# Feed-forward lots of 2, 6, 6 and 8 tiles: both lots of six go down by seven block products, the first lot over all eight banks

## The chip, the cores and the metric

The kernel runs on one core of one Trainium2 chip. The metric is the device time of one execution in microseconds. Before the change it was 1090.71 us (median of three runs, 1090.43 to 1090.75).

## The reference

The reference is a two-layer transformer trunk on one sequence of 512 tokens, 1024 wide, with a memory of 256 rows. Each layer is a token mixer with memory attention, and then a feed-forward part of hidden width 2816. All inputs are fp32, and layer 1 has another mixer than layer 0. What the change touches is the feed-forward part:

```
for i in range(DEPTH):                       # 2 layers
    ...                                      # mixer A (i = 0) or B (i = 1), memory attention, W_o
    h = rms_norm(x, g_ffn_pre[i])
    gu = h @ w_gate_up[i]                    # 512x1024 @ 1024x5632
    f = (jax.nn.silu(gu[..., :D_FF]) * gu[..., D_FF:]) @ w_down[i]   # D_FF = 2816
    x = x + rms_norm(f, g_ffn_post[i])
```

## The kernel before

An fp32 number is held as two rounded parts, hi and lo, in a format that TensorE (PE) multiplies fast; each product of matrices is three matmuls, hi by hi, hi by lo and lo by hi (`mm3`, lines 307 to 309). Every weight block is loaded as fp32 into a raw buffer by a DMA on SyncE's queue (SP) and split on the chip: ScalarE (ACT) rounds the hi part (`split`, line 317), VectorE (DVE) subtracts it to get the lo part (line 321). Such a block of 128x1024 is called a unit (`unit`).

The hidden width is cut into 22 tiles of 128 (f = 0 to 21). Tiles 0 and 1 compute gate and up as plain products. Every other tile does so by seven block products instead of eight (Strassen's scheme with Winograd's sums, `seven`, lines 1143 to 1145), each matmul 128x256; `prep_a` to `prep_d` and `load_b` load, add and split the weights for them one to three tiles ahead. For the "far" tiles some of the weight sums are made by DMAs that GpSimd (POOL) issues with an accumulate (`load_far`, `add`), which saves DVE work.

The hidden tiles are multiplied with `w_down` in lots: `LOTS` = tiles 0 to 7, 8 to 13 and 14 to 21, and each lot's result is added to `o` (four tiles of 128x1024, in SBUF). The lots go down in three ways:

- lot 0 (eight tiles): `Trunk.down`, eight products per token tile for each half of the output columns, in four banks of PSUM at a time, 192 matmuls of 128x512 (the first of them between the lot's last gate/up products); ACT copies the result to `o`.
- lot 1 (six tiles, `SEVEN` = 1): `down` in `ffn`, seven block products A11, A12, S2, S1, S3, S4, A22 in this order, by `times` (lines 1255 to 1257), 126 matmuls of 128x512. Its weights come as blocks b11, b12, b21, b22 of `ws`, 128x1536 each, in two pieces (1024 columns in `raw`, `ru` or `rb`, 512 in `rs`). The sums t1 to t4 of blocks are made by loads on SP and accumulates of POOL (`load_block`, `add`, line 1091). `down_load` issues all of them in four steps: 0 and 1 while the lot's last tiles run, 2 at the start, 3 after product A12. `pairs` splits a block for PE, `out_of` adds a finished product to `o` on DVE (line 1265).
- the last lot (eight tiles): `ffn_out`, 192 matmuls again, with the post norm.

`ahead` is called eight times in `Trunk.down` (after each unit) and four times in `ffn_out`. It takes one item of a list `todo`, a weight unit that the next layer's mixer will need, loads and splits it and, at the next call, stores both parts to DRAM (`pair`). In the next layer `unit` fetches the parts instead of loading and splitting again. The list has eight items (four of `wq`, then four of `wo`). It is filled in layer 0 before the feed-forward; six items are prepared in layer 0, and the two left over are prepared in layer 1's first lot, where nothing uses them.

PE's instructions run in the order of the program text. The order on the other engines and on the DMA queues is chosen by a scheduler at build time and is fixed in the program; `queue` ties one DMA behind the last one that was tied on the same queue (`issue_after`). Each engine works strictly in that order: an instruction that waits holds up everything behind it on its engine, and a DMA that waits to be issued holds up its queue.

Of the kernel before, what the change touches and what calls it, by code (L numbers as in the profile page):

```python
# [9 lines left out]
F32 = mybir.dt.float32  # L10
# [6 lines left out]
P = 128  # L17
# [43 lines left out]
def _pack(w_in, w_mem_kv, w_o, w_gate_up, w_down):  # L61
    wkv = np.empty((DEPTH, 4, P, 768), np.float32)
    wq = np.empty((DEPTH, 4, 2, P, 1024), np.float32)
    wm = np.empty((DEPTH, 4, P, 1024), np.float32)
    wo = np.empty((DEPTH, 2, KD // 2, P, 1024), np.float32)
    wgu = np.empty((DEPTH, NF, 2, P, 1024), np.float32)
    wd = np.empty((DEPTH, 2, NF // 2, P, 1024), np.float32)
    ws = np.empty((DEPTH, 2, 2, P, HALF * 512), np.float32)
    qk = NH * HD + NG * HD
    cols = (np.arange(0, qk, HD)[:, None] + AXIAL[None, :]).reshape(-1)  # L70
    w_in = w_in.copy()
    w_in[1, :, :qk] = w_in[1][:, cols]
    for l in range(DEPTH):
        for u in range(4):
            wkv[l, u] = _unit_layout(w_in[l], 2 * u, 2, 768, 384)
            wm[l, u] = _unit_layout(w_mem_kv[l], 2 * u, 2, 0, 512)
        for c in range(4):
            c0 = 256 * c if c < 3 else 1152
            for u in range(2):
                wq[l, c, u] = _unit_layout(w_in[l], 4 * u, 4, c0, 256)  # L80
        for h in range(2):
            for u in range(KD // 2):
                wo[l, h, u] = _unit_layout(w_o[l], 2 * u, 2, 512 * h, 512)
            for u in range(NF // 2):
                wd[l, h, u] = _unit_layout(w_down[l], 2 * u, 2, 512 * h, 512)
            for z in range(2):
                ws[l, z, h] = _unit_layout(w_down[l], LOTS[SEVEN][0] + HALF * z, HALF, 512 * h, 512)
# [115 lines left out]
class Trunk:  # L203
# [492 lines left out]

    def axial(self, buf):
# [4 lines left out]
        nc.sync.dma_start(buf[:, :2 * NT * HD], a["ropeb"])  # L702
        nc.sync.dma_start(buf[:, 2 * NT * HD:2 * NT * HD + 2 * HD], _rows(a["qk_norm_g"], 2 * HD))
        nc.gpsimd.tensor_scalar(g[:, 0], g[:, 0], -(HD ** -0.5), 1.0, op0=OP.mult, op1=OP.mult)
        for z in range(2):
            nc.gpsimd.tensor_mul(self.gt[:, z, 0], rt[:, 0], g[:, z, None, :].to_broadcast([P, NT, HD]))
            for h in range(2):
                o, i = slice(32 * h, 32 * h + 32), slice(32 - 32 * h, 64 - 32 * h)
                nc.gpsimd.tensor_mul(self.gt[:, z, 1, :, o], rt[:, 1, :, o],
                                     g[:, z, None, i].to_broadcast([P, NT, 32]))  # L710

# [187 lines left out]

    def down(self, get, w, fs, c, o, head=None):  # L900

        nc = self.nc
        for h in range(2):
            ps = head["ps"] if h == 0 else [self.tagged(z) for z in ("s", "pv", "acc", "acc")]
            for u in range(len(fs) // 2):
                wu = head["w"] if (h, u) == (0, 0) else self.unit(w[h, fs[0] // 2 + u])
                for t in range(0 if h or u else 2, NT):
                    self.down_prod(ps[t], get, fs, u, t, wu)
                self.ahead()
            for t in range(NT):  # L910
                z = o[t][:, 512 * h:512 * h + 512]
                if c == 0:
                    nc.scalar.activation(z, ps[t], AF.Copy)
                else:
                    nc.vector.tensor_add(z, z, ps[t])

    def down_prod(self, ps, get, fs, u, t, wu):
# [78 lines left out]
    def ffn(self, l, pools, forms, late, done):  # L996
# [26 lines left out]
        def keep_hidden(f, s, i, lot):  # L1023
            p = F[f] = hidden(i)
            a, b = slice(0, 256), slice(256, 512)
            if lot != SEVEN or i >= HALF:
# [20 lines left out]

            if lot == SEVEN:
                forms_due.append(low if i < HALF else high)
# [4 lines left out]

        def block(name, z, i, t):
            f0 = LOTS[SEVEN][0]
# [7 lines left out]
        def product(f):  # L1064
            if f < 2:
                return o[2 + f][:, :512]
            return temp("k" if 0 <= f - LOTS[SEVEN][0] < HALF else "s")

# [17 lines left out]
        def far(f):  # L1086
            return 1 < f - LOTS[SEVEN][0] < 2 * HALF

# [160 lines left out]

        def times(ps, name, pr, steps, fresh):  # L1250
            mm = nc.tensor.matmul
            for i, t in steps:
                lh, ll = block(name, 0, i, t), block(name, 1, i, t)
                rh, rl = [pr[i // 2][z][:, i % 2 * 512:i % 2 * 512 + 512] for z in range(2)]
# [12 lines left out]
        def down_load(h, step):  # L1267
            (b11, b12), (b21, b22) = [[self.a["ws"][l, z, n] for n in range(2)] for z in range(2)]
            if step == 0:
# [12 lines left out]
        def down_begin(h):  # L1282
            h["x"] = [self.tagged("acc"), self.tagged("acc")]
            h["w"] = pairs(h["b11"])
            down_load(h, 2)
            times(h["x"], "A11", h["w"], BY_UNIT[:4], True)

        def down(h):
# [10 lines left out]
            times(x, "S2", w, BY_UNIT, False)  # L1299
# [6 lines left out]
            times(x, "S3", w, BY_ROW, False)  # L1306
            out_of(x, 1, 1, True)
            w = pairs(h["b22"])
            times(y, "S4", w, BY_ROW, False)
            out_of(y, 0, 1)  # L1310
            w = pairs(h["t4"])
            times(x, "A22", w, BY_ROW, False)
            out_of(x, 1, 0)

        for c, (f0, f1) in enumerate(LOTS):
            fs = list(range(f0, f1))
            get = lambda z, k, t, f0=f0: F[f0 + k][z][:, t * P:(t + 1) * P]
            gs = [f for f in fs if f >= 2]
            if c:
                prep_a(gs[0])  # L1320
# [8 lines left out]
            prep_d(gs[0])  # L1329
            head = {}  # L1330

            def begin(nxt, nxt2):
                if c == SEVEN and nxt == fs[-1]:
                    down_load(head, 1)
                if c == SEVEN and nxt2 == fs[-1]:
                    down_load(head, 0)

            def first():
                if c == SEVEN:
                    down_begin(head)  # L1340
                    return
# [4 lines left out]
            def second():  # L1346
                if c == SEVEN:
                    times(head["x"], "A11", head["w"], BY_UNIT[4:], True)
                    return
# [6 lines left out]
            if c == SEVEN:  # L1356
# [225 lines left out]
```

## Time and profile before

The profile is of one execution of 1090.64 us; the span from its first to its last instruction is 1088.9 us, so 1.7 us lie outside the span.

| what | measured |
|---|---|
| median of three runs | 1090.71 us |
| profiled execution, its span | 1090.64 us, 1088.9 us |
| PE, DVE, ACT, POOL busy | 1066.2, 867.5, 677.5, 228.7 us |
| feed-forward lot 0, layer 0 and 1 | 104.42 and 101.16 us |
| feed-forward lot 1 (six tiles), layer 0 and 1 | 86.30 and 86.32 us |

How to read it: PE stands for matmuls, SPq for SyncE's DMA queue, a row of the timeline is the start, the length, the engine, the line of the program, the operation and out<-in. In the view of waits a row names who waited for what, then the microseconds in all, how often, and the longest. In a view of DMAs the last number is the median time from issue to landing. Times are counted from the start of the span.

### The profile page before, as it was taken

Reading aid. Unit: us, or ns where it says so; the run is one execution under the profiler, and the core shown is the slowest. Engines: PE = TensorE matmul, PEld = TensorE weight load, DVE = VectorE, ACT = ScalarE, POOL = GpSimd, SP = SyncE. Lnnn points to the kernel's source line nnn. Section 1 sums busy time; section 2 is a strip of 40 time slices with the busy share of each in tenths; the row PEclk is TensorE's granted clock in tenths of the full one; section 3 lists DMA queues with packets and bytes.
Section 4 is the critical chain, followed back from the end, with each engine's and each line's share of the span. In section 5 each row is a group of like instructions: output and inputs, shape, how many; then the busy total and the mean of one; then the engine's idle time right before and its main releaser. Section 6 shows DMA issues by size and latency. Waiting matters only on the chain.

```text
span 1088.9 us, 19743 instructions
## 1 busy us (share of the span) xinstructions
PE 1066.2 (98%) x7400; PEld 976.6 (90%) x7400; DVE 867.5 (80%) x1489; ACT 677.5 (62%) x1393; POOL 228.7 (21%) x373
## 2 busy tenths in 40 slices
PE   9999999999999999999999999999999999999997
PEld 7899878999789989997898888778999899899986
DVE  7789875999557989985888988767997468899954
ACT  7679974765445646654567888756664356556631
POOL 5773331102001100001444543312000001100001
PEclk9999999999999999999999999999999999999999
DMA  9721007333865972338732220145135648833243
GB/s 337 255 78 39 23 20 264 124 98 129 268 205 146 259 204 89 117 118 305 240 131 97 78 78 20 59 154 193 62 117 204 182 117 248 226 117 101 72 158 116
DMA packets 48624, 159.23 MB, mean 146 GB/s; under 512 B 5649, under 2 KB 6033, under 8 KB 48401
## 3 DMA queue, kind: packets, MB, share of 16 engines
q1 hardware_dynamic: 43632, 147.09, 40.0%
q0 software_dynamic: 4608, 10.49, 5.6%
q8 instruction: 58, 0.95, 0.4%
q10 hardware_dynamic: 288, 0.40, 0.1%
q14 instruction: 38, 0.30, 0.1%
HBM read 135.94 MB, written 18.87 MB: 142 GB/s over the span
## 4 chain that ended last, share of the span: by engine, by line
PE 78%; DVE 9%; ACT 5%; DMA 3%; issue 2%; POOL 2%; SPq 0%; DVEq 0%; POOLq 0%; ACTq 0%
PE ps L1144 11%; PE ps L1143 11%; PE ps L1145 11%; PE ps L308 10%; PE ps L307 10%; PE ps L309 10%; PE tp L672 3%; PE ps L1257 2%; PE ps L1256 2%; PE ps L1255 2%; PE o L686 2%; PE o L687 2%; DVE wlo L321 2%; ACT whi L317 1%; PE s L611 1%
## 5 line engine op out<-in xcount | busy, mean ns | idle before, releaser
L317 ACT ACTIVATE whi<-raw 128x512 fp32r<-128x512 f32 (+3 forms) x198 | 159.9, 826 | 122.5 <-DMA pair<-whi 30.3
L321 DVE TENSOR_TENSOR wlo<-raw,whi 128x512 fp32r<-128x512 f32 (+3 forms) x194 | 180.0, 943 | 64.0 <-ACT whi L317 59.7
L1144 PE MATMUL ps<-hrows,wlo 128*128 128x256 f32 x640 | 176.3, 276 | 0.0
L1143 PE MATMUL ps<-hrows,whi 128*128 128x256 f32 x640 | 176.2, 275 | 0.0
L1145 PE MATMUL ps<-hrows,whi 128*128 128x256 f32 x640 | 176.2, 275 | 0.0
L307 PE MATMUL ps<-whi,hrows 128*128 128x256 f32 (+2 forms) x432 | 143.8, 333 | 0.0
L308 PE MATMUL ps<-wlo,hrows 128*128 128x256 f32 (+2 forms) x432 | 137.7, 319 | 1.6 <-DVE wlo L321 1.6
L309 PE MATMUL ps<-whi,hrows 128*128 128x256 f32 (+2 forms) x432 | 137.6, 319 | 0.0
L1143 PE MATMUL ps<-a,whi 128*128 128x256 f32 x480 | 132.2, 275 | 0.5 <-DVE c L1179 0.5
L1144 PE MATMUL ps<-a,wlo 128*128 128x256 f32 x480 | 132.1, 275 | 0.0
L1145 PE MATMUL ps<-a,whi 128*128 128x256 f32 x480 | 132.1, 275 | 0.0
L1143 PEld LDWEIGHTS ps<-hrows,whi 128*128 128x128 f32 x640 | 120.1, 188 | 0.5
L1144 PEld LDWEIGHTS ps<-hrows,wlo 128*128 128x128 f32 x640 | 120.1, 188 | 0.5
L1145 PEld LDWEIGHTS ps<-hrows,whi 128*128 128x128 f32 x640 | 120.1, 188 | 0.0
L308 PE MATMUL ps<-wlo,f 128*128 128x512 f32 (+1 forms) x264 | 101.6, 385 | 2.4 <-DVE wlo L321 2.4
L307 PE MATMUL ps<-whi,f 128*128 128x512 f32 (+1 forms) x264 | 101.3, 384 | 0.3 <-ACT whi L317 0.3
L309 PE MATMUL ps<-whi,f 128*128 128x512 f32 (+1 forms) x264 | 101.1, 383 | 0.0
L662 POOL TENSOR_SCALAR p<-p,rd 128x256 f32<-128x256 f32 (+2 forms) x128 | 78.2, 631 | 101.4 <-DVE rd L659 59.3
L1143 PEld LDWEIGHTS ps<-a,whi 128*128 128x128 f32 x480 | 90.1, 188 | 0.9 <-DVE c L1179 0.7
L1144 PEld LDWEIGHTS ps<-a,wlo 128*128 128x128 f32 x480 | 90.1, 188 | 0.2
L1145 PEld LDWEIGHTS ps<-a,whi 128*128 128x128 f32 x480 | 90.1, 188 | 0.0
L308 PEld LDWEIGHTS ps<-wlo,hrows 128*128 128x128 f32 x432 | 81.4, 188 | 7.5 <-DVE wlo L321 2.5
(229 smaller groups left out, 2663.2 us busy)
## 6 DMA issues: line engine op xcount, KB each, us to landing
raw<-in_wgu_dram SPq DMA_DIRECT2D x48, 512.0 KB, 4.5
rb<-in_wgu_dram SPq DMA_DIRECT2D x40, 512.0 KB, 3.7
raw<-in_wd_dram SPq DMA_DIRECT2D x32, 512.0 KB, 4.8
raw<-in_wo_dram SPq DMA_DIRECT2D x18, 512.0 KB, 3.6
raw<-in_wq_dram SPq DMA_DIRECT2D x16, 512.0 KB, 4.9
xt<-x SPq DMA_DIRECT2D x12, 512.0 KB, 5.0
raw<-in_wm_dram SPq DMA_DIRECT2D x8, 512.0 KB, 4.2
x<-y SPq DMA_DIRECT2D x8, 512.0 KB, 2.9
```

Source lines behind the costliest of these rows:

```text
L307: mm(out, lh, rh, start=first, stop=False)
L308: mm(out, lh, rl, start=False, stop=False)
L309: mm(out, ll, rh, start=False, stop=last)
L317: a = nc.scalar.activation(hi, src, AF.Copy)
L321: b = nc.vector.tensor_sub(lo, src, hi.bitcast(F32))
L662: self.pooled = nc.gpsimd.tensor_scalar(hd["p"][z][:, :n], hd["p"][z][:, :n], rd[:, z:z + 1], 1.0, op0=OP.mult, op1=OP.mult)
L672: nc.tensor.transpose(tp[:, z], hd["p"][i][:, jj * P:(jj + 1) * P], self.ident)
L686: nc.tensor.matmul(o[:, c0:c1], hd["v"](j), th, start=(j == 0), stop=False, skip_group_check=True)
L687: nc.tensor.matmul(o[:, c0:c1], hd["v"](j), tl, start=False, stop=last, skip_group_check=True)
L1143: mm(out, wh[:, s], rh, start=start and k == 0, stop=False, skip_group_check=True)
L1144: mm(out, wl[:, s], rh, start=False, stop=False, skip_group_check=True)
L1145: mm(out, wh[:, s], rl, start=False, stop=k == 3, skip_group_check=True)
```

## The change

The lots become tiles 0 and 1, 2 to 7, 8 to 13 and 14 to 21, and both lots of six go down by seven products. `ws` holds the blocks of both.

The new first lot is done at once behind the plain tiles. It needs two units of `w_down`, one for each half of the columns, which are loaded and split while the plain tiles run (`w0`). Its 48 matmuls go over all eight banks of PSUM, four token tiles by two halves, tile 0 first and tile 1 after it, and ACT copies the eight results to `o`. The preparation of tile 2 (`prep_a(2)`) and the second half of the token sums (`forms.finish(1)`) stand after the plain tiles now. `Trunk.down` is gone.

With it go eight of the calls of `ahead`. In their place `down` calls a new function `spare` twice, after step 3 of `down_load` and after product S1. The first call takes an item of `todo`, queues its load on SP into a raw buffer behind what is queued there, and splits it in two halves (into `c` and `s`, buffers of 128x512 that the gate/up tiles use otherwise); the second queues the four stores. In layer 0's first way down by seven the first call also queues two loads of the rope tables for layer 1 (`axial`, which stood behind lot 0 before). The four calls in `ffn_out` stay. So four items are prepared in layer 0 and four in layer 1, the last two of those in `ffn_out`.

```diff
-LOTS = ((0, 8), (8, 14), (14, 22))
-SEVEN, HALF = 1, 3
+LOTS = ((0, 2), (2, 8), (8, 14), (14, 22))
+SEVEN, HALF = (1, 2), 3
...
             act(f, pgs[f])
             if f == 0:
+                raw0 = wide("ru")
+                nc.sync.dma_start(raw0, self.a["wd"][l][0, 0])
+                w0 = [self.unit(self.a["wd"][l][0, 0], raw=raw0)]
                 forms.finish(0)
-                prep_a(2)
-                forms.finish(1)
+                w0.append(self.unit(self.a["wd"][l][1, 0]))
+        prep_a(2)
+        forms.finish(1)
+        get = lambda z, k, t: F[k][z][:, t * P:(t + 1) * P]
+        ps = [[self.tagged(z) for z in tags.split()] for tags in ("t t acc acc", "s s s pv")]
+        for k in range(2):
+            c = slice(512 * k, 512 * k + 512)
+            for h in range(2):
+                for t in range(NT):
+                    self.mm3(ps[h][t], get(0, k, t), get(1, k, t), w0[h][0][:, c], w0[h][1][:, c], k == 0, k == 1)
+        for h in range(2):
+            for t in range(NT):
+                nc.scalar.activation(o[t][:, 512 * h:512 * h + 512], ps[h][t], AF.Copy)
...
+        def spare():
+            if l == 0 and "rope" not in turn:
+                turn["rope"] = 1
+                self.axial(tmp.tile([P, 10 * HD], F32, tag="rope", name="rope", bufs=1), queue, ends)
+            if self.stores:
+                for dst, src in self.stores:
+                    queue(nc.sync, dst, src)
+                self.stores = []
+            elif self.todo:
+                name, *at = self.todo.pop(0)
+                x = self.wraw.tile([P, 1024], F32, tag="raw", name="raw", bufs=3)
+                queue(nc.sync, x, self.a[name][tuple(at)])
...
+                for z in range(2):
+                    c = slice(512 * z, 512 * z + 512)
+                    hi, lo = temp("c"), temp("s")
+                    self.split(hi.bitcast(F32R), lo.bitcast(F32R), x[:, c])
+                    self.stores += [(y[0][:, c], hi), (y[1][:, c], lo)]
...
-            times(z, "A12", w, BY_UNIT, True)
+            times(z, h, "A12", w, BY_UNIT, True)
             down_load(h, 3)
+            spare()
             out_of(z, 0, 0)
...
-            times(y, "S1", w, BY_ROW, True)
+            times(y, h, "S1", w, BY_ROW, True)
+            spare()
             out_of(y, 1, 1)
...
             if c == SEVEN:
                 down(head)
-            elif c < len(LOTS) - 1:
-                self.down(get, self.a["wd"][l], fs, c, o, head)
-                if l == c == 0:
-                    self.axial(wide("ru"))
```

(The last `if` reads `if c in SEVEN` now, as its like elsewhere.) In the changed kernel the line numbers move: the splits of DVE are line 322, the loads of `queue` line 1079, `out_of` line 1267, the three matmuls of `times` lines 1257 to 1259.

The first place where the order moves is SP's queue at the end of a lot of six. Before, in layer 0, from the last loads of `ws` on (`raw<-in_wgu` and `rb<-in_wgu` are for the next lot's tiles; the last `rs` is the second half of b22, the row ahead of it b22's first half or t4):

```order
L1091 DMA rb<-in_ws_dram 128x1024
L1109 DMA raw<-in_wgu_dram 128x1024 x3
L1091 DMA rs<-in_ws_dram 128x512
L1091 DMA rb<-in_ws_dram 128x1024
L1091 DMA rs<-in_ws_dram 128x512
L1091 DMA rb<-in_ws_dram 128x1024
L1091 DMA rs<-in_ws_dram 128x512
L1113 DMA rb<-in_wgu_dram 128x1024 x4
```

After, the same place of the second lot of six in layer 0:

```order
L1079 DMA rb<-in_ws_dram 128x1024
L1079 DMA rs<-in_ws_dram 128x512
L1079 DMA rb<-in_ws_dram 128x1024
L1079 DMA rs<-in_ws_dram 128x512
L1079 DMA rb<-in_ws_dram 128x1024
L1079 DMA rs<-in_ws_dram 128x512
L1079 DMA raw<-in_wq_dram 128x1024
L1097 DMA raw<-in_wgu_dram 128x1024 x2
L1079 DMA pair<-c 128x512
L1101 DMA rb<-in_wgu_dram 128x1024
```

The three loads for the next lot no longer stand among the `ws` loads; the spare's load and two of them stand behind the last one. In layer 1 both lots of six read the same way (with `wo` for `wq`); in layer 0's first lot of six the two rope loads stand between the last `rs` and the spare's load.

The second place is DVE during the way down, from the split of t3 (`wlo<-rb`, `wlo<-rs`) to that of b22. Before, in layer 0:

```order
L321 TENSOR_TENSOR wlo<-rs,whi 128x512
L1265 TENSOR_TENSOR o<-o,ps 128x512 x2
L321 TENSOR_TENSOR wlo<-rb,whi 128x1024
L321 TENSOR_TENSOR wlo<-rs,whi 128x512
L1265 TENSOR_TENSOR o<-o,ps 128x512 x2
L321 TENSOR_TENSOR wlo<-rb,whi 128x1024
L321 TENSOR_TENSOR wlo<-rs,whi 128x512
L1265 TENSOR_TENSOR o<-o,ps 128x512
```

After, in the second lot of six of layer 0 (`s<-raw,c` are the spare's two half splits):

```order
L322 TENSOR_TENSOR wlo<-rs,whi 128x512
L1267 TENSOR_TENSOR o<-o,ps 128x512 x2
L322 TENSOR_TENSOR wlo<-rb,whi 128x1024
L322 TENSOR_TENSOR s<-raw,c 128x512 x2
L1267 TENSOR_TENSOR o<-o,ps 128x512
L322 TENSOR_TENSOR wlo<-rs,whi 128x512
L1267 TENSOR_TENSOR o<-o,ps 128x512
L322 TENSOR_TENSOR wlo<-rb,whi 128x1024
L322 TENSOR_TENSOR wlo<-rs,whi 128x512
L1267 TENSOR_TENSOR o<-o,ps 128x512
```

The spare's splits stand ahead of the second half of t3, which product S3 reads in its third step. In layer 1 both lots of six have the same order; in layer 0's first lot of six the spare's splits stand behind both halves of t3 and ahead of b22.

More of the change, by code (lines that the diff above doesn't have):

```diff
@@ L695, in value, with axial @@
         nc.vector.tensor_add(self.tok[here, hg // 2], o[here], tmp[here])
-    def axial(self, buf):
+    def axial(self, buf, queue, ends):
         nc, a = self.nc, self.a
@@ L701, in axial @@
         g = buf[:, 2 * NT * HD:2 * NT * HD + 2 * HD].rearrange("p (z d) -> p z d", d=HD)
[L702 to L704 removed]
+        queue(nc.sync, buf[:, :2 * NT * HD], a["ropeb"])
+        queue(nc.sync, buf[:, 2 * NT * HD:2 * NT * HD + 2 * HD], _rows(a["qk_norm_g"], 2 * HD))
+        with self.tc.issue_after(ends[nc.gpsimd]):
+            last = nc.gpsimd.tensor_scalar(g[:, 0], g[:, 0], -(HD ** -0.5), 1.0, op0=OP.mult, op1=OP.mult).ins
         for z in range(2):
[L706 removed]
+            with self.tc.issue_after(last):
+                last = nc.gpsimd.tensor_mul(self.gt[:, z, 0], rt[:, 0], g[:, z, None, :].to_broadcast([P, NT, HD])).ins
             for h in range(2):
                 o, i = slice(32 * h, 32 * h + 32), slice(32 - 32 * h, 64 - 32 * h)
[L709 to L710 removed]
+                with self.tc.issue_after(last):
+                    last = nc.gpsimd.tensor_mul(self.gt[:, z, 1, :, o], rt[:, 1, :, o],
+                                                g[:, z, None, i].to_broadcast([P, NT, 32])).ins
+        ends[nc.gpsimd] = last
     def mixer(self, l, mkp, late, tokp):
@@ L898, in mix_out @@
         return late
[L900 to L915, printed above, removed]
     def down_prod(self, ps, get, fs, u, t, wu):
@@ L1025, in keep_hidden @@
             a, b = slice(0, 256), slice(256, 512)
-            if lot != SEVEN or i >= HALF:
+            if lot not in SEVEN or i >= HALF:
                 self.flo = signed(p, slice(0, 512), s)
@@ L1046, in high @@
                 signed(F["S4", q // 2], (a, b)[q % 2], r[:, a])
-            if lot == SEVEN:
+            if lot in SEVEN:
                 forms_due.append(low if i < HALF else high)
@@ L1053, in due, with block @@
                 forms_due.pop(0)()
-        def block(name, z, i, t):
-            f0 = LOTS[SEVEN][0]
+        def block(lot, name, z, i, t):
+            f0 = LOTS[lot][0]
             key, h = {"A11": (f0 + i, 0), "S3": (f0 + i, 1), "A12": (f0 + HALF + i, 0), "A22": (f0 + HALF + i, 1),
@@ L1086, in far @@
         def far(f):
-            return 1 < f - LOTS[SEVEN][0] < 2 * HALF
+            return any(1 < f - LOTS[c][0] < 2 * HALF for c in SEVEN)
         def queue(eng, *args, **kw):
@@ L1248, in pairs, with times @@
             return out
-        def times(ps, name, pr, steps, fresh):
+        def times(ps, h, name, pr, steps, fresh):
             mm = nc.tensor.matmul
             for i, t in steps:
-                lh, ll = block(name, 0, i, t), block(name, 1, i, t)
+                lh, ll = block(h["lot"], name, 0, i, t), block(h["lot"], name, 1, i, t)
                 rh, rl = [pr[i // 2][z][:, i % 2 * 512:i % 2 * 512 + 512] for z in range(2)]
@@ L1267, in down_load @@
         def down_load(h, step):
-            (b11, b12), (b21, b22) = [[self.a["ws"][l, z, n] for n in range(2)] for z in range(2)]
+            (b11, b12), (b21, b22) = [[self.a["ws"][l, SEVEN.index(h["lot"]), z, n] for n in range(2)] for z in range(2)]
             if step == 0:
@@ L1285, in down_begin @@
             down_load(h, 2)
-            times(h["x"], "A11", h["w"], BY_UNIT[:4], True)
+            times(h["x"], h, "A11", h["w"], BY_UNIT[:4], True)
+        def spare():
[10 more added lines that the diff above has]
+                queue(nc.sync, x, self.a[name][tuple(at)])
+                self.pairs[(name, *at)] = y = [self.dram.tile([P, 1024], F32, name="pair", tag="_".join(map(str, (name, z, *at))))
+                                               for z in range(2)]
+                for z in range(2):
[3 more added lines that the diff above has]
+                    self.stores += [(y[0][:, c], hi), (y[1][:, c], lo)]
         def down(h):
@@ L1329, in ffn @@
             prep_d(gs[0])
-            head = {}
+            head = dict(lot=c)
             def begin(nxt, nxt2):
-                if c == SEVEN and nxt == fs[-1]:
+                if c in SEVEN and nxt == fs[-1]:
                     down_load(head, 1)
-                if c == SEVEN and nxt2 == fs[-1]:
+                if c in SEVEN and nxt2 == fs[-1]:
                     down_load(head, 0)
             def first():
-                if c == SEVEN:
+                if c in SEVEN:
                     down_begin(head)
@@ L1346, in second @@
             def second():
-                if c == SEVEN:
-                    times(head["x"], "A11", head["w"], BY_UNIT[4:], True)
+                if c in SEVEN:
+                    times(head["x"], head, "A11", head["w"], BY_UNIT[4:], True)
                     return
```

23 lines of the change are left out of this document (12 added, 11 removed).

## The prediction, on record before the result was known

> **What bounds the kernel now.** I read the page's busy times, its clock line and the chain of waits first.
>
> ```profile
> span 1088.9 us, 19743 instructions
> PE 1066.2 (98%) x7400; PEld 976.6 (90%) x7400; DVE 867.5 (80%) x1489; ACT 677.5 (62%) x1393; POOL 228.7 (21%) x373
> PEclk9999999999999999999999999999999999999999
> PE 78%; DVE 9%; ACT 5%; DMA 3%; issue 2%; POOL 2%; SPq 0%; DVEq 0%; POOLq 0%; ACTq 0%
> ```
>
> TensorE (PE) sets the end: 98% busy at full clock, 78% of the chain. A matmul less is worth its pitch, as long as VectorE (DVE), ScalarE (ACT) and the loads keep up. So I went to the stages that change. The view of windows gives, in this order, the first lot and the lot of six in layer 0, then the same two in layer 1, then the last 14 us of the plain tiles and the six-tile lot's way down in layer 0.
>
> ```profile
> core 0: us, PE busy (x) PEld busy (x) DVE busy (x) ACT busy (x) POOL busy (x), PEclk, DMA share, GB/s
> 220.97:325.39 104.42, 102.05 (x699) 93.39 (x698) 78.54 (x102) 51.87 (x82) 9.44 (x10) 1.00 0.57 183
> 325.39:411.69 86.30, 86.30 (x632) 80.80 (x632) 72.38 (x113) 50.40 (x84) 11.42 (x13) 1.00 0.73 196
> 774.32:875.48 101.16, 101.16 (x699) 93.34 (x698) 74.47 (x100) 50.61 (x80) 2.68 (x3) 1.00 0.49 154
> 875.48:961.80 86.32, 86.32 (x632) 80.80 (x632) 71.58 (x113) 50.41 (x84) 11.48 (x13) 1.00 0.72 196
> 207.00:221.00 14.00, 14.00 (x125) 14.00 (x124) 14.00 (x23) 11.39 (x19) 0.00 (x0) 1.00 0.13 39
> 387.00:411.70 24.70, 24.70 (x110) 20.15 (x109) 23.03 (x34) 11.59 (x16) 2.67 (x3) 1.00 0.64 173
> ```
>
> Both lots of six tiles take 86.3 us with PE never idle. The first lot of layer 0 loses 2.4 us (104.42 against 102.05 busy); the waits of PE in that window name most of it:
>
> ```profile
> PE ps L308 <- DVE wlo L321: 1.6, 2, 0.8
> PE ps L1143 <- DVE c L1179: 0.5, 1, 0.5
> PE ps L307 <- ACT whi L317: 0.3, 1, 0.3
> ```
>
> **The change, part by part.** *The first lot.* Today it is six seven-way tiles plus 192 matmuls of 128x512 down. It becomes 48 such matmuls for tiles 0 and 1, and six tiles that go down as the lot of six does now. One such matmul costs, from the first and last starts of the lot of six's way down in PE's timeline (108 matmuls of lines 1255 to 1257 between the first row and the last, which begins the next lot):
>
> ```profile
> 386.74 0.39 PE L1255 MATMUL ps<-whi,f 128*128 128x512 f32 x1
> 411.53 0.28 PE L1143 MATMUL ps<-a,whi 128*128 128x256 f32 x1
> ```
>
> (411.53 - 386.74)/108 = 0.2295 us. The 48 take 48 x 0.2295 = 11.0 us, and the six tiles another 86.3: 97.3 us in place of 104.42 (layer 0: -7.1) and of 101.16 (layer 1: -3.9), **-11.0 us** together. By count it is 36 matmuls less, 36 x 0.2295 = 8.3 us; the other 2.7 us are layer 0's stalls and slack inside the windows. The 48 need two weight splits more on DVE. What covers them: DVE is full before the lot (14.00 of 14.00 us), but the 11.0 us of matmuls need no other DVE work, so the backlog that now sits ahead of tile 2 has that time to drain. The eight copies to `o` are ACT's, which was busy 51.87 of 104.42 us. I take no stall there. Without the cover it is at most the two splits, 2 x 1.22 us per layer (the 128x1024 split is quoted below).
>
> *The spare work inside the sevens.* This is the dear part. Eight next-layer weight units used to be pre-split between the units of the ordinary way down; now `spare` does one inside each way down by seven products. The order shows that the load of the spare unit (`raw<-in_wq`) stands on SP right behind `rs<-in_ws`, the second half of block b22. Today that row waits on SP for a long time: the waits of SP (layer 0, then layer 1), and the rows of SP, PE, POOL and the DMA view around it.
>
> ```profile
> SPq L1091 <- DMA rs<-rs: 11.1, 1, 11.1
> SPq L1091 <- DMA rs<-rs: 11.9, 1, 11.9
> 383.79 0.33 SPq L1091 DMA_DIRECT2D rb<-in_ws_dram  x1
> 385.92 0.33 SPq L1091 DMA_DIRECT2D rs<-in_ws_dram  x1
> 386.34 0.39 SPq L1091 DMA_DIRECT2D rb<-in_ws_dram  x1
> 397.94 0.33 SPq L1091 DMA_DIRECT2D rs<-in_ws_dram  x1
> 949.32 0.33 SPq L1091 DMA_DIRECT2D rs<-in_ws_dram  x1
> 949.75 2.03 SPq L1113 DMA_DIRECT2D rb<-in_wgu_dram  x2
> 936.84 0.39 PE L1255 MATMUL ps<-whi,f 128*128 128x512 f32 x1
> 391.04 0.88 POOL L1091 DMA_DIRECT2D rb<-ru  x1 [0.29 <-DVE k L1043]
> 391.85 0.99 POOL L1091 DMA_DIRECT2D rs<-rs  x1
> rs<-rs POOLq DMA_DIRECT2D x1, 256.0 KB, 5.9
> ```
>
> SP stands from 386.7 to 397.94 for the last accumulate of block t4 (issued by POOL at 391.85, 5.9 us to landing: 397.8). In layer 1 it ends at 949.32, which is 399.2 on layer 0's time line (both lots begin their ways down 550.10 apart: 936.84 and 386.74). Today nothing urgent is queued behind it. After the change the spare's load is, and DVE, which works in order, has the spare's two splits ahead of the second half of t3's split. PE needs that half in the third step of S3. On DVE and ACT today:
>
> ```profile
> 394.00 0.69 DVE L321 TENSOR_TENSOR wlo<-rs,whi 128x512 fp32r<-128x512 f32 x1
> 397.75 0.68 DVE L1265 TENSOR_TENSOR o<-o,ps 128x512 f32<-128x512 f32 x1
> 400.10 1.22 DVE L321 TENSOR_TENSOR wlo<-rb,whi 128x1024 fp32r<-128x1024 f32 x1
> 400.69 0.64 ACT L317 ACTIVATE whi<-rs 128x512 fp32r<-128x512 f32 x1 [0.77 <-DMA rs<-in_ws_dram]
> 400.88 0.39 PE L1256 MATMUL ps<-wlo,f 128*128 128x512 f32 x1
> 403.60 0.39 PE L1256 MATMUL ps<-wlo,f 128*128 128x512 f32 x1
> ```
>
> Let L be the landing of the spare's load. In three of the four ways down (layer 0's second lot of six, both of layer 1) DVE's chain behind L is: ACT's half 0.64, two half splits 0.69 and 0.60 (back to back they follow 0.60 apart), one addition 0.60, t3's half 0.69, and about 0.1 of hand-over: L + 3.3. PE wants it at 400.88 (third step of S3, second matmul). Stall: L + 3.3 - 400.88. In layer 0's first lot of six t3's half comes ahead of the spare, and what is late is b22's first half, wanted at 403.60 (second matmul of S4): 0.64 + 0.69 + 0.60 + two additions 1.28 + 1.22 = 4.4, so L + 4.4 - 403.60.
>
> Now L. Let T be the time at which b22's row is released. Floor: 394.7, because its buffer is one that DVE frees at 394.69 (first row above). Ceiling: today's 397.9 to 399.2. What moves it: the three loads of 512 KB that SP puts between `ws` loads today go behind b22's row after the change, and the stretch in which they compete is a full one:
>
> ```profile
> 368.61 10.26 SPq L1109 DMA_DIRECT2D raw<-in_wgu_dram  x3
> raw<-in_wgu_dram SPq DMA_DIRECT2D x3, 512.0 KB, 7.8
> rb<-in_wgu_dram SPq DMA_DIRECT2D x1, 512.0 KB, 3.8
> ```
>
> These loads took 7.8 us each there, against 3.8 us for the same size in a quiet place (at 949.75, right behind a 256 KB load, as the spare will be). POOL starts t4's first accumulate at 391.04, 7.2 us after the load that it adds to was issued (383.79). If that load takes 3.8 us, and the 0.6 us to POOL's start stay, POOL starts at 388.2, 2.8 us earlier, and the last accumulate lands at 397.8 - 2.8 = 395.0. I take **T = 395.0**, near the floor, since the loads that crowd it are gone. Then L = T + 0.43 (SP's next row, as 949.75 - 949.32) + 3.8 = 399.25, and the stall is 399.25 + 3.3 - 400.88 = 1.7 us, three times: 5.1. In layer 0's first lot of six two rope loads stand between (two rows of SP, 0.9, and a share of the engines, an estimate 0.4): L = 400.5, stall 1.3. Sum **+6.4 us**. From both ends: T at the floor, 394.7, gives 5.2; T as late as today, 397.9 in layer 0 and 399.2 in layer 1, gives 4.6 + 4.2 + 5.9 + 5.9 = 20.6; below, if the load lands 1.7 us sooner after its issue than the quiet row, about 0.
>
> The Trainium skill, page "DMA: Bandwidth & Descriptors", section "Anatomy of one DMA — SWDGE (gpsimd) path", fits a transfer by 2.0 us plus bytes/436e3. By it 256 KB would take 2.6 us and 512 KB 3.2 us, so that T would sit at its floor and L 0.6 earlier than mine; the sum for the spares would be about 2.7, and the whole 1083.7, the first rival's time. The trace disagrees for the accumulate (5.9 us) and is 0.6 above it for the load (3.8 us), and I go by the trace.
>
> The same page, section "Issuing engines are not separate DMA queues", says that transfers from SP and GpSimd end on the same 16 engines and interleave; by it the deferral must bring the accumulates forward, and it speaks against the third rival below.
>
> *The rest.* Fewer units are pre-split for layer 1 (four in layer 0 instead of six): layer 1 splits two units of the output projection itself, each 1.22 us of DVE and about that on ACT, in a stage where PE waits for DVE only now and then: 0 to 2.4, taken +0.4. What is left on the list is prepared without use in layer 1: two of it in the last lot's way out, between its units. In layer 0 that sits there today and PE waits for it once; in layer 1, with nothing left by then, never. The waits of PE from 505 to 525:
>
> ```profile
> PE ps L308 <- DVE wlo L321: 0.9, 1, 0.9
> ```
>
> So **+1.0** (0 to 1.5). DVE does not become the bound of a lot of six by this: 72.38 of 86.30 us busy today, and with the spare's two half splits 73.8.
>
> Sum against the profiled execution (1090.64 us, span 1088.9): 1090.64 - 11.0 + 6.4 + 0.4 + 1.0 = **1087.4 us**. The median of the runs shown is 1090.71, 0.07 above that execution, which changes nothing.
>
> **The rivals.** *The spare is hidden* (0.18). T at its floor and the load quicker behind an emptied queue, or the splits find their place: +0 to 3 in place of 6.4, so 1081 to 1084. For it: DVE has 14 us of slack in each such lot; against it: DVE is 23.03 of 24.70 busy just in the way down. *T does not move* (0.22). The accumulates are slow by themselves, so that SP is released as late as today and the spares cost up to 20.6: 1090.64 - 11.0 + 20.6 + 1.4 = 1101.6 at the most; it is slower than before once the four stalls pass 9.6 (11.0 less 1.4), that is from T of about 395.8 on, and by over 0.2% from 396.4. For it: 5.9 us for 256 KB with no load of SP's issued in the 5 us before. Against it: they wait for loads that landed late in a crowd. I put its middle at 1096. *DVE becomes the bound elsewhere* (0.10): the plain tiles' backlog is not drained and both first lots lose their gain in part: 2 x 1.22 per layer on top, 1090 to 1092.
>
> **How the numbers follow.** Forecast 0.50, its own range 1084.5 to 1090.5. 0.2% (2.2 us) is about what a measurement tells from no change: faster is below 1088.5, slower above 1092.9. The forecast gives 0.34 faster and 0.16 same; the hidden spare 0.18 faster; T unmoved 0.20 slower and 0.02 same; DVE 0.07 same, 0.03 slower. Together 0.52, 0.25, 0.23. The range leaves out one in ten on each side: 1082.5 to 1096.
>
> **What would show it.** In the waits of PE: a wait of 1 to 2.5 us in each of the four ways down by seven, in the second product line (wlo) of S3 (of S4 in the first), released by DVE; SP's b22 row at T = 394.7 to 396 (8 to 9 us after the first A12 matmul); the windows of the first lot 97.3 plus that stall. It is wrong if PE does not wait there, if SP's row still comes 11 us and more after A12's start, or if PE waits at the start of the feed-forward.

## The result, and the profile after

The changed kernel takes 1100.4 us (median of four runs, 1097.81 to 1101.15) against 1090.57 on the same chip: 1.0086 times as long, 95% interval 1.0069 to 1.0104. I had forecast 1087.4, between 1082.5 and 1096. Its profiled execution took 1100.04 us, with this page:

```profile
span 1098.3 us, 20016 instructions
PE 1065.9 (97%) x7364; PEld 973.1 (89%) x7364; DVE 899.5 (82%) x1567; ACT 697.7 (64%) x1435; POOL 251.8 (23%) x405
PEclk9999999999989999999999999999999999999999
PE 75%; DVE 9%; DMA 6%; ACT 4%; issue 2%; POOL 2%; SPq 0%; DVEq 0%; POOLq 0%; ACTq 0%
```

PE has 36 matmuls less and is busy for nearly as long as before (1066.2 us): a slice of the clock line shows an 8, so some of its matmuls ran slowly. DMA has gone from 3% to 6% of the chain. The view of windows names the places; the rows are the 48 matmuls of the new first lot in layer 0, then the four ways down by seven in order of time (layer 0 twice, layer 1 twice):

```profile
core 0: us, PE busy (x) PEld busy (x) DVE busy (x) ACT busy (x) POOL busy (x), PEclk, DMA share, GB/s
222.03:232.94 10.91, 10.91 (x50) 9.02 (x49) 9.65 (x14) 7.07 (x12) 1.93 (x2) 1.00 0.65 163
294.46:326.72 32.26, 27.38 (x110) 21.54 (x109) 24.34 (x36) 10.86 (x17) 7.23 (x11) 0.89 0.77 246
388.25:417.88 29.63, 26.69 (x111) 21.27 (x110) 24.50 (x36) 12.44 (x18) 2.50 (x3) 0.94 0.78 231
853.38:882.01 28.63, 26.72 (x110) 21.29 (x109) 24.75 (x36) 12.39 (x18) 2.95 (x4) 0.94 0.90 257
943.53:971.41 27.88, 25.39 (x110) 20.04 (x109) 23.03 (x34) 12.39 (x18) 2.18 (x3) 1.00 0.84 245
```

The 48 matmuls take 10.91 us with PE never idle, as forecast. A way down by seven took 24.8 us before (411.53 - 386.74) and takes 32.26, 29.63, 28.63 and 27.88 now: 7.5 + 4.8 + 3.8 + 3.1 = **19.2 us** too much, and in three of them the granted clock is below 1. What PE waits for there, from its waits:

```profile
PE ps L1258 <- DVE wlo L322: 8.1, 4, 2.9
PE ps L1257 <- DVE o L1267: 4.0, 1, 4.0
```

Measured as the distance of two matmul starts less one pitch, the waits are 5.95 us in the first way down (S4, in three pieces: 4.17, 1.41, 0.37), 3.10 in the second, 2.08 and 2.56 in layer 1 (S3): 13.7 in all. Of the other 5.5, 5.0 us are in the three ways down whose clock is below 1, as matmuls at half clock; 0.5 are in the fourth, at full clock, in short gaps right behind the wait and at the start of A22.

The chain behind the second one, in layer 0, in the wait of SP and the rows of SP, ACT, DVE and PE (A12 begins at 388.25 here):

```profile
SPq L1079 <- DMA rs<-rs: 9.3, 1, 9.3
397.87 0.33 SPq L1079 DMA_DIRECT2D rs<-in_ws_dram  x1
398.26 0.41 SPq L1079 DMA_DIRECT2D raw<-in_wq_dram  x1
402.29 1.15 ACT L318 ACTIVATE c<-raw 128x512 fp32r<-128x512 f32 x2 [4.67 <-DMA raw<-in_wq_dram]
402.95 1.29 DVE L322 TENSOR_TENSOR s<-raw,c 128x512 fp32r<-128x512 f32 x2 [4.19 <-ACT c L318]
404.76 0.68 DVE L322 TENSOR_TENSOR wlo<-rs,whi 128x512 fp32r<-128x512 f32 x1
405.50 0.50 PE L1258 MATMUL ps<-wlo,f 128*128 128x512 f32 x1 [2.94 <-DVE wlo L322]
```

SP's row for b22 waits 9.3 us for t4's last accumulate (`rs<-rs`) and is released at 397.87, the spare's load stands right behind it and lands at 402.27; ACT has then stood for 4.67 us and DVE for 4.19. DVE does the spare's two half splits, an addition, and only then the half of t3 that PE has been waiting for.

### The profile page after: what moved, and what is told of

The parts are those of the page before. It is cut to its first block, busy times and chain, and to the rows that moved or that the text cites. A ratio compares the mean times of both kernels' runs of the same rounds, so it can differ in the third digit from the quotient of the medians.

```text
span 1098.3 us, 20016 instructions
## 1 busy us (share of the span) xinstructions
PE 1065.9 (97%) x7364; PEld 973.1 (89%) x7364; DVE 899.5 (82%) x1567; ACT 697.7 (64%) x1435; POOL 251.8 (23%) x405
## 4 chain that ended last, share of the span: by engine, by line
PE 75%; DVE 9%; DMA 6%; ACT 4%; issue 2%; POOL 2%; SPq 0%; DVEq 0%; POOLq 0%; ACTq 0%
PE ps L1131 11%; PE ps L1132 11%; PE ps L1133 11%; PE ps L309 8%; PE ps L308 8%; PE ps L310 8%; PE tp L673 3%; PE ps L1258 2%; PE ps L1259 2%; PE ps L1257 2%; DVE wlo L322 2%; PE o L687 2%; DMA rs<-rs 2%; PE o L688 2%; PE s L612 1%
## 5 line engine op out<-in xcount | busy, mean ns | idle before, releaser
L318 ACT ACTIVATE whi<-raw 128x512 fp32r<-128x512 f32 (+3 forms) x186 | 145.8, 803 | 99.6 <-issue 24.7
L322 DVE TENSOR_TENSOR wlo<-raw,whi 128x512 fp32r<-128x512 f32 (+3 forms) x182 | 162.7, 910 | 37.1 <-ACT whi L318 36.5
L310 PEld LDWEIGHTS ps<-whi,hrows 128*128 128x128 f32 x432 | 81.1, 188 | 5.5 <-DVE hrows L336 0.3
L308 PEld LDWEIGHTS ps<-whi,hrows 128*128 128x128 f32 x432 | 81.3, 188 | 5.1
L318 ACT ACTIVATE whi<-rb 128x1024 fp32r<-128x1024 f32 x56 | 59.5, 1063 | 27.0 <-PE ps L1259 18.5
```

The lines of the kernel that those rows point to most:

```text
L308: mm(out, lh, rh, start=first, stop=False)
L310: mm(out, ll, rh, start=False, stop=last)
L318: a = nc.scalar.activation(hi, src, AF.Copy)
L322: b = nc.vector.tensor_sub(lo, src, hi.bitcast(F32))
```

## The experiments

The theory after the result: the waits come from the spare's load, which stands behind a row of SP that waits for t4's last accumulate; and where PE stands long enough, the clock is halved for a while on top. The rivals: DVE is just too full in the way down; the new lots themselves cost the time; the slow matmuls have another cause. All ratios are to the kernel of before on the same chip (the chip of the experiments ran that kernel in 1091.5 to 1092.6 us, so times are compared by ratio, stages by the profile). The ways down are those of the one profiled execution; of the kernels with `q` alone and without spare work in layer 1 that was the fastest of ten.

| kernel | us | ratio (95%) | four ways down, us |
|---|---|---|---|
| changed | 1100.40 | 1.0086 (1.0069 to 1.0104) | 32.3, 29.6, 28.6, 27.9 |
| b22's half in `q` | 1087.76 | 0.996 (0.9947 to 0.9974) | 27.1, 24.8, 24.8, 24.8 |
| no spare | 1085.41 | 0.9943 (0.9924 to 0.9962) | 25.9, 24.8, 24.8, 24.8 |
| no spare in layer 1 | 1094.83 | 1.0027 (1.0015 to 1.0039) | 33.1, 29.9, 24.8, 24.8 |
| matmuls in the waits | 1115.35 | 1.022 (1.0197 to 1.0242) | 33.3, 35.0, 32.0, 31.0 |
| spare between S3 and S4 | 1101.52 | 1.0072 (1.0055 to 1.0088) | 33.0, 29.0, 27.1, 29.5 |
| b22's halves swapped | 1101.05 | 1.0088 (1.0068 to 1.0107) | 32.1, 26.5, 29.3, 26.3 |
| rope loads behind the spare | 1097.13 | 1.0041 (1.0021 to 1.006) | 28.2, 30.2, 31.2, 27.7 |
| `q`, rope, layer 1 together | 1085.28 | 0.9935 (0.9922 to 0.9947) | 24.8, 24.9, 24.8, 24.8 |

**Taking the wait on the accumulate away.**

```diff
-                m, rs = wide("rb"), tmp.tile([P, 512], F32, tag="rs", name="rs", bufs=4)
+                m, rs = wide("rb"), temp("q")
```

> The changed kernel (1100.4 us), but the second half of block b22 is loaded into the buffer `q` instead of an `rs` buffer, so its row on SP waits for DVE alone and no longer for the last accumulate of t4. Queue theory (the spare's load comes late because it stands behind that row): the row is released about 6 us after A12 begins instead of 8.9 to 10.0, the spare's load lands about 10.5 us after A12's start, PE no longer waits in S3 in three of the four ways down (under 0.5 us each), at most 1 us is left in layer 0's first one (rope loads in between), and the clock stays at 1.0: 19.2 us of excess go to 0 to 2, the time is 1081 to 1084 us. Rival (DVE is simply too full there with two more half splits, whenever the load lands): 1.2 to 2 us of wait stay in each way down, 1086 to 1092 us.

In the second way down SP's rows now read so (A12 begins at 381.88):

```profile
387.79 0.33 SPq L1079 DMA_DIRECT2D q<-in_ws_dram  x1
388.18 0.68 SPq L1079 DMA_DIRECT2D raw<-in_wq_dram  x1
```

The row is released 5.9 us after A12's start instead of 9.6, three ways down are back at 24.8 us and the first is at 27.1. DVE does the same 1567 instructions as in the changed kernel and PE does not wait in three ways, so the rival falls: DVE is not simply too full. But two things differ here and not one. The scheduler also laid DVE's order out anew and put the second half of t3 ahead of the spare's splits:

```profile
392.30 0.68 DVE L322 TENSOR_TENSOR wlo<-rs,whi 128x512 fp32r<-128x512 f32 x1
393.98 1.29 DVE L322 TENSOR_TENSOR s<-raw,c 128x512 fp32r<-128x512 f32 x2 [0.99 <-ACT c L318]
```

The load lands 11.4 us after A12's start; with the order of the changed kernel the prediction's formula would still leave 11.4 + 3.3 - 14.14 = 0.6 us of wait. What the new order does without the early release is shown below, by the spare between S3 and S4. The first way down keeps 2.3 us, where I had expected at most 1. The profiled execution, 1083.66 us, lies in the range that I wrote, but it is the fastest of ten; the median, 1087.76, is 4 us above that range, on a chip where the kernel of before also takes 1 us more. By ratio it is 0.4% faster. Where the other 4 us of the slower executions lie is not shown.

**No spare work.** The two branches of `spare` that load, split and store are switched off; the rope loads stay.

```diff
-            if self.stores:
+            if l < 0 and self.stores:
...
-            elif self.todo:
+            elif l < 0 and self.todo:
```

> The changed kernel without the spare's load, splits and stores; the two rope loads stay where they are, ffn_out prepares two units in layer 0, layer 1's mixer loads and splits the other six itself. Queue theory: all four ways down take 24.8 us as before (19.2 us less), and layer 1's mixer pays at most some 1 to 3 us for four more splits than in the changed kernel: 1081 to 1085 us. Rival (the first lot's new form or the second way down by seven itself costs the time): the ways down stay above 26 us, 1090 us or more.

The lots themselves cost nothing: three ways down take 24.8 us. The first takes 25.9, where I had expected 24.8; it waits 1.0 us in A22, and the rope loads are still in it. The time is 0.4 us above my range. What the spare work saves is seen in layer 1's mixer: from the last lot's end in layer 0 to layer 1's first lot this kernel, with two units prepared, takes 243.59 us and the changed one, with four, 241.57. (The last kernel below, with four, takes 244.16, but 1.7 us of that are a stretch at half clock.)

**No spare work in layer 1**, where nothing uses it.

```diff
-            elif self.todo:
+            elif self.todo and l == 0:
```

> The changed kernel without the spare work in layer 1, where its results are never used. Queue theory: layer 1's two ways down fall from 28.63 and 27.88 us to 24.8 (6.9 us less), layer 0's stay at 32.3 and 29.6: 1093 to 1095 us. Rival (the waits in layer 1 come from the ws loads themselves being late): the two stay above 26.5 us, 1097 us or more.

As the queue theory says: layer 1's ways down are at 24.8 us, layer 0's are not, and the ratio falls from 1.0086 to 1.0027. Six tenths of a per cent went into units that no layer reads.

**Keeping PE busy in the waits.** 

```diff
+                late = l == 0 and h["lot"] == SEVEN[0]
+                if t == 0 and (i == 0 and name == "S4" if late else i == HALF - 1 and name == "S3"):
+                    fill, f = self.tagged("s"), F[LOTS[h["lot"]][0]][0]
+                    for _ in range(16 if late else 8):
+                        mm(fill, f[:, :P], f, start=True, stop=True, skip_group_check=True)
```

> The changed kernel with 8 more matmuls of 128x512 (1.84 us, results unused, own bank) on PE right ahead of the matmul that waits in S3, and 16 (3.7 us) ahead of S4 in layer 0's first way down; all of them fit into the waits seen (2.1 to 5.6 us). Clock theory (PE standing still for 2 us and more halves the granted clock for some 3 to 7 us after it): the clock stays at 1.0, about 5 us of the 19.2 go, 1094 to 1096.5 us although PE does more. Rival (the slow matmuls after the waits have another cause, such as crowded DMA engines): the clock dips as before, 1099 to 1101.5 us.

The time is far above both ranges, and this tells nothing on the clock. With more matmuls on PE the scheduler laid DVE's order out anew: waits of 3.7 and 3.5 us turned up in A22 in the second and fourth way down, and in the third S3 still waited 3.2 us, so PE lost more than before. The question went to the next pair.

**Holding PE in a quiet place.** The kernel of before, with four holds in layer 1's `ffn_out`; `n` is 2, 4, 3, 6 in the first and 3, 5, 2, 4 in the second kernel (one execution of each, 1106.78 and 1104.93 us).

```diff
+        def hold(n):
+            b = self.tagged("t")
+            for z in range(2):
+                nc.tensor.matmul(b, get(0, 0, 0), wu0[0][:, :512], start=True, stop=True)
+                for _ in range(n if z == 0 else 0):
+                    nc.scalar.activation(self.junk(), b, AF.Copy)
```

> The kernel of before with four holds of PE in layer 1's last stage: a matmul, n reads of its bank by ACT, and a matmul that has to wait for them; n = 2, 4, 3, 6, so waits of some 1.5, 2.7, 2.1, 3.9 us. Clock theory: after the waits above 2 us the granted clock is halved for 3 us or more (1.5 us or more lost behind each), after 1.5 us it stays at 1.0. Rival (crowded DMA engines are what slows PE): no dip, since few loads run there.

> The same with n = 3, 5, 2, 4, so waits of some 2.1, 3.3, 1.5, 2.7 us at the same four places: if the length of the wait decides, the dips move with it; if the place does, they stay at the places where gate_a shows them.

The holds lasted 1.5, 2.8, 2.2, 4.1 us and 2.1, 3.4, 1.5, 2.8 us. The clock was halved behind the second and the fourth in one kernel, behind the first alone in the other: behind 2.1 us, but not behind 2.2, 3.4 and one of the two of 2.8. So neither length nor place decides alone, and both theories fall as I wrote them. In the changed kernel the low clock lasts 3.4 us or twice that, and its starts lie on a grid: 313.87, 406.03 and 870.25, and 92.16 is 27 times 3.413, 464.2 is 136 times 3.413. Cut along that grid (the first two views to within about 0.1 us), the windows of the changed kernel (its second and fourth way down), of the first and the second kernel with holds, and then of the last kernel below and of the one without spare work, both in mixers:

```profile
402.60:406.00 3.40, 0.50 (x2) 0.46 (x3) 3.04 (x6) 2.31 (x4) 0.00 (x0) 1.00 1.00 309
406.00:409.40 3.40, 3.40 (x9) 2.67 (x9) 2.55 (x5) 0.51 (x1) 0.00 (x0) 0.51 0.98 348
955.50:958.90 3.40, 2.33 (x11) 1.59 (x9) 1.22 (x3) 1.89 (x3) 0.00 (x0) 1.00 1.00 373
958.90:962.30 3.40, 2.07 (x9) 1.73 (x10) 3.40 (x6) 0.73 (x2) 0.00 (x0) 1.00 0.89 268
```

```profile
1056.80:1060.20 3.40, 0.76 (x3) 0.49 (x3) 0.00 (x0) 2.44 (x5) 0.00 (x0) 0.98 0.00 0
1060.20:1063.60 3.40, 3.40 (x10) 2.66 (x9) 1.91 (x2) 1.20 (x2) 0.00 (x0) 0.51 0.00 0
1070.40:1073.80 3.40, 2.47 (x11) 1.69 (x10) 0.69 (x1) 0.80 (x2) 0.00 (x0) 1.00 0.00 0
1073.80:1077.20 3.40, 2.33 (x10) 1.95 (x11) 0.87 (x2) 1.71 (x4) 1.18 (x2) 1.00 0.00 0
```

```profile
1043.90:1047.31 3.41, 1.46 (x7) 0.97 (x6) 0.68 (x2) 2.40 (x4) 0.00 (x0) 1.00 0.77 252
1047.31:1050.72 3.41, 3.41 (x10) 2.63 (x9) 1.23 (x1) 0.45 (x1) 0.00 (x0) 0.50 0.99 386
1057.55:1060.96 3.41, 1.87 (x9) 1.22 (x7) 0.00 (x0) 1.38 (x3) 0.00 (x0) 1.00 0.00 0
1060.96:1064.37 3.41, 1.68 (x7) 1.41 (x8) 0.05 (x1) 2.67 (x4) 0.00 (x0) 1.00 0.00 0
```

```profile
532.26:535.67 3.41, 1.55 (x8) 1.05 (x7) 1.85 (x3) 1.46 (x3) 1.14 (x2) 1.00 0.61 238
535.67:539.09 3.42, 3.42 (x15) 3.33 (x14) 2.64 (x3) 1.66 (x5) 1.57 (x4) 0.50 0.74 269
128.25:131.66 3.41, 1.89 (x14) 1.46 (x12) 2.98 (x9) 3.39 (x13) 1.13 (x3) 1.00 0.09 18
131.66:135.07 3.41, 3.41 (x12) 2.92 (x11) 2.48 (x8) 2.48 (x8) 1.09 (x2) 0.50 0.34 136
```

The number behind POOL's is the granted clock, the two behind it are the DMA share and the rate. Where PE was busy 0.50, 0.76, 1.46 or 1.55 us of a window, the next window runs at half clock; behind 1.68, 1.87 and more in the kernels with holds it does not. PE's busy time gives no sharp border: in the first mixer of the kernel without spare work, in a part of the program that the change leaves as it was, the clock was halved behind 1.89 us. A hold of 3.4 us that falls across two windows (1.87 and 1.68 busy) costs nothing more; one of 2.1 us inside one window costs 3.4 us at half clock, 1.7 us of matmuls. In the first of the two kernels the DMA engines move nothing in the halved window and the one ahead of it (share 0.00), so crowded engines are not the cause.

The Trainium skill, page "TensorE: Matmul & The Clock Gate", section "What's actually happening", gives a free-running activity window of 3413 ns after which the clock is set to half or full; these rows agree with it. Its section "HAM oscillation — how this bites in real kernels" gives as a rule that PE must not idle for more than some 3.4 us; here 2.1 us inside a window was enough and 3.4 us across two was not, and the measurement decides.

**The order on DVE.** The spare's calls moved between S3 and S4, and behind A22.

```diff
             down_load(h, 3)
-            spare()
...
             w = pairs(h["b22"])
+            spare()
             times(y, h, "S4", w, BY_ROW, False)
```

> The changed kernel with the spare's first call between S3 and S4 in the program, its second behind A22: the load stays where it was in SP's queue, but on DVE the spare's splits now stand behind both halves of t3 and one addition, ahead of b22's. Queue theory: S3 no longer waits; S4 waits for b22's lo part, 0.5 to 1.2 us in three ways down (25.3 to 26.0 us each in place of 29.63, 28.63, 27.88) and without a drop of the clock; layer 0's first one stays near 32; 1090 to 1093 us. Rival (the order on DVE does not matter, only the load's landing does): the three stay at 27.5 us or more, 1098 us or more.

My expectation fell. S3 no longer waits, but the time is no better (1.0072, within the interval of the changed kernel). In the second way down PE waits like this instead:

```profile
PE ps L1258 <- DVE wlo L322: 2.5, 2, 1.4
PE ps L1257 <- ACT whi L318: 0.8, 1, 0.8
```

S4 waits for b22's hi half on ACT and for its lo half on DVE, and A22 for t4. The spare's load still lands late, and what stands behind its splits on the two engines, b22's, is late with it; I had counted DVE's queue and left ACT's out. A22 waits by another path: on DVE the split of t4 stands behind additions for the next lot, and the first of these waits 1.41 us for a load (`rb<-in_wgu`) that SP issues behind the spare's load. In the fourth way down A22's wait, 2.8 us, is the only one. So the order on DVE alone does not help while the row is released late (9 to 11 us after A12's start here); with the early release and t3 ahead of the spare, in the kernel with `q`, the waits of three ways are gone.

**What sets the release of b22's row.**

```diff
-                h["b22"] = load_block(m, b22, rs=rs)
+                queue(nc.sync, rs, b22[:, 1024:])
+                queue(nc.sync, m, b22[:, :1024])
+                h["b22"] = [m, rs]
```

> The changed kernel with the two halves of block b22 in the other order on SP: the 512 KB half, which today starts just ahead of POOL's last accumulates, goes behind the row that waits for them. It tells why that row was released at 8.9 to 10.0 us after A12's start and not at 8.3 as I forecast. If SP's load and the accumulates share the DMA engines, the accumulates (7.1 and 6.6 us in the changed kernel's second way down of layer 0) get shorter by what 512 KB takes there, and the release comes 0.7 to 1.5 us earlier in each way down; if the accumulates are slow by themselves, it stays within 0.2 us. The time itself need not fall: the spare's load now has 512 KB more ahead of it (1098 to 1104 us).

POOL's three accumulates in layer 0's second way down, issue to landing, in the changed kernel and then here:

```profile
rb<-ru POOLq DMA_DIRECT2D x1, 512.0 KB, 7.1
rs<-in_ws_dram POOLq DMA_DIRECT2D x1, 256.0 KB, 5.5
rs<-rs POOLq DMA_DIRECT2D x1, 256.0 KB, 6.6
```

```profile
rb<-ru POOLq DMA_DIRECT2D x1, 512.0 KB, 5.5
rs<-in_ws_dram POOLq DMA_DIRECT2D x1, 256.0 KB, 4.1
rs<-rs POOLq DMA_DIRECT2D x1, 256.0 KB, 4.8
```

The release comes 8.1, 7.9, 9.3 and 7.2 us after A12's start in place of 10.0, 9.6, 8.9 and 9.3: earlier by 1.9, 1.7 and 2.1 us in three of them, more than I expected, and later by 0.4 in layer 1's first, where POOL could issue the last accumulate only 5.9 us after A12's start (3.3 in the changed kernel). SP's 512 KB and the accumulates share the engines; with that load out of the way these three are 1.4 to 1.8 us shorter each. The time, 1101.05 us, is in the range that I wrote.

**The rope loads.** `axial` is called in the branch that queues the stores.

```diff
-            if l == 0 and "rope" not in turn:
...
             if self.stores:
+                if l == 0 and "rope" not in turn:
```

> The changed kernel with the two rope loads queued behind the spare's load (with its stores) in layer 0's first way down. If they alone make that way the worst one, its spare load lands 4.0 to 4.4 us after SP's release instead of 7.7, it takes 28 to 30 us like the other three instead of 32.3, and the time falls by 2 to 4 us to 1096 to 1098; if the place of that lot in the program is to blame, it stays above 31.5 us.

In layer 0's first way down (A12 at 293.24):

```profile
302.71 0.33 SPq L1079 DMA_DIRECT2D rs<-in_ws_dram  x1
303.09 0.42 SPq L1079 DMA_DIRECT2D raw<-in_wq_dram  x1
303.56 0.42 SPq L1079 DMA_DIRECT2D rope<-in_ropeb_dram  x1
```

The spare's load lands 4.4 us after the release (7.7 before) and the way down takes 28.2 us instead of 32.3. DVE's order changed with it: PE waits 2.9 us in S3 now, as in the other three ways, and not in S4. The time is what I expected (1097.13 us; by ratio 1.0041 against 1.0086). Two of the other ways down were slower in this profile (30.2 and 31.2); their row was released 10.2 to 10.3 us after A12's start, later than in the changed kernel.

**All three together**: the buffer `q`, the rope loads behind the spare, no spare work in layer 1.

> The changed kernel with b22's second half in the buffer `q`, the two rope loads moved behind the spare's first unit (to its second call), and no spare work in layer 1. Queue theory: each of the three causes of waiting is gone, all four ways down take 24.8 us as the one of before (q22 alone left 27.12 in the first, with the rope loads), layer 1's first gate/up after them waits no more; 1081 to 1083 us, 0.7 to 0.9% below before on the same chip. Rival (rope is not what was left in the first way down): it stays at 26.5 us or more and the time 1083 to 1086 us.

```profile
span 1083.1 us, 19989 instructions
PE ps L309 <- DVE wlo L322: 2.2, 3, 0.9
PE ps L308 <- ACT whi L318: 1.3, 1, 1.3
PE ps L1131 <- ACT p L1137: 1.2, 2, 0.9
```

All four ways down are at 24.8 to 24.9 us and the waits of `times` are gone from PE's list; the kernel is 0.65% faster than before (0.53 to 0.78%); I had written 0.7 to 0.9% and 1081 to 1083 us, and it takes 1085.28. Of the three waits shown, the first is an old one (line 308 before, 4.0 us in all). The other two are new at this size: 1.3 us at the passage to layer 1's mixer, where the clock is halved once more (535.67 to 539.09, shown above), and 1.2 us at the first gate/up tile behind a way down. I did not pursue them. Against the kernel without any spare work (0.9943, 0.9924 to 0.9962) this one is not measurably better, so no gain is shown from the spare work of layer 0, even where it is hidden.

## Why the prediction was wrong

*The first lot* was right: -11.0 us. Without the excess of its way down, layer 0's first two lots take 104.69 - 7.46 = 97.2 us and layer 1's (780.95 to 882.01) 101.06 - 3.83 = 97.2, where I had 97.3. The backlog of DVE ahead of it did drain.

*The place and the mechanism of the stall* were right: second matmul of S3's third step in three ways down, S4 in the first, released by DVE, behind the spare's load, behind b22's row. *Its length as a function of the release* was right too: with the release 9.62 us after A12's start and 4.4 to the landing, L + 3.3 - 400.88 is 9.62 + 4.4 + 3.3 - 14.14 = 3.2; measured 3.10. In layer 1, with 8.91 + 4.1 and 9.29 + 4.2, it gives 2.2 and 2.65; measured 2.08 and 2.56. None of the three signs of being wrong that I named came: the row was released at 8.9 to 10.0 us, between the 8 to 9 of the forecast and the 11 of the sign.

**The step that failed is T.** I put the release at 395.0, 8.26 us after A12's start, by moving POOL's issues 2.8 us ahead and keeping the last accumulate's 5.9 us. That put the last issue 2.3 us after A12's start. In the second way down POOL's issues did move (2.5 to 3.3 us ahead, the last one to 2.6), but the accumulates got longer: 6.6 us for the last, since they now overlapped the 512 KB half of b22 that SP issues 0.4 us ahead of A12, as the swapped halves show. In the other three both parts of the sum differ: in the first way the last accumulate took 5.9 us as I had kept it, but was issued only at 4.0; in layer 1 it was issued at 3.3 and 2.5 and took 5.5 and 6.7. Released at 8.9 to 10.0, the row let the four stalls grow to 13.7 us from the 6.4 of the forecast. In the first way the rope loads add to that: with them the spare's load landed 7.7 us behind the release instead of 5.5, and the 0.4 us that I gave them as their share of the engines came from no row. I had also counted only one half of the first way's limit: S4 writes the bank that the two additions read, so it already waits at its first matmul.

**The term that was missing is the clock**: 5.0 us, and 0.5 of short gaps. I counted a stall at its length. Three of the four put PE's busy time in a window below half (0.80, 0.53 and 1.50 us of 3.41), and up to two windows behind ran at half clock.

*The rest*: I added 1.0 for the useless units in layer 1's `ffn_out` and got none (114.44 us from the last lot's start to the end of its 128x512 matmuls in both kernels); I added 0.4 for layer 1's mixer and got 0.9. Layer 0 came 1.2 us later to its feed-forward part; 0.8 of it is lost at 20 to 31 us, in the first mixer, where the program is unchanged, and the kernel with `q` does not show it (from PE's first matmul to the first lot 219.63 us, as before; 220.86 in the changed kernel). The sum is 1090.64 - 11.0 + 13.7 + 5.5 + 1.2 = 1100.04; the last 1.2 is what remains of these 1.2 and 0.9, since the last lot of layer 0 and the end of the program come out some 0.4 us shorter each. Two slips in the prediction change no term: by the fit that it quotes, L would come 0.9 us earlier and not 0.6 (its 2.7 and 1083.7 are worked out with 0.9; the section quoted is on DMAs that GpSimd issues, and the spare's load is SP's), and the rival that the shared engines speak against is the second, "T does not move".

Of the rivals, "T does not move" had the sign and nearly the size, with a release that moved by 1.2 to 3.6 us and still too little: its point of decision, four stalls of more than 11.8 us for a loss that can be measured, was passed. That its upper end, 1101.6, lies so near the result is luck: it stands for stalls of 20.6 us and no clock, and the stalls were 13.7.

## What to carry to other kernels

Before a load is queued anywhere, look at the row ahead of it on that queue and at what that row waits for; filler work whose data can come late also blocks each engine that is to process it in order, so it has to be hidden on all of them at once. A transfer's time taken from a profile is good for the company it had there: when issues move, who shares the engines changes. And in these runs a stall of PE near 2 us was dearer than its length, by 1.7 us, where it fell inside one window of the clock's grid.

## What the runs showed of the hardware

- In these traces the clock changes on a fixed grid of 3.41 us, and a window in which PE was busy for less than about half is followed by one at half clock (1.46 and 1.55 us halved, 1.68 not; once 1.89 halved, so the border is not sharp). The same wait can cost 0 or 1.7 us more by where it falls; that fits the changed kernel's spread of 1097.81 to 1101.15 us at mean clocks of 0.995 to 0.992, though I did not trace those runs one by one.
- An accumulate of 256 KB between two places in SBUF took 3.3 to 8.5 us from issue to landing in these runs, and one of 512 KB 4.6 to 8.2 us; the swapped halves show that what else is in flight is part of it. A plain load of 256 KB, b22's second half behind its long wait, took 2.5 to 2.9.
